# Batch norm over 32 x 256 x 128 x 128: the next load waits for VectorE, the next store for ScalarE

## The chip, the cores and the metric

The kernel runs on one core of a Trainium2 chip. The metric is the device time of one execution in microseconds (us), and the median of several runs is compared. Before the change it is 2484.73 us.

## What is computed

Batch normalisation with given statistics: a factor and an offset for each of 256 channels, applied to 32 images of 128 x 128.

```python
x:  (32, 256, 128, 128) float32        # 536.9 MB
gamma, beta, running_mean, running_var: (256,) float32

return gamma * (x - mean) / np.sqrt(var + eps) + beta     # eps = 1e-5, per channel
```

With `scale = gamma / sqrt(var + eps)` and `shift = beta - mean * scale`, each output is `x * scale + shift`. Each byte of `x` is read once and each byte of the result written once: 1073.7 MB in all.

## The kernel before

**Tiles.** `x` is cut into 64 tiles (32 images x 2 blocks of 128 channels). A tile has 128 partitions, one per channel, with 16384 columns of float32: 64 KB a partition, 8.39 MB in all. Three buffers (`NBUF = 3`) of that size lie in the on-chip memory, and tile i uses buffer i mod 3. A tile is loaded, changed in place, and stored from the same buffer.

**Loads** are issued by the sync engine (SP), on its own ring of DMA descriptors (q1 in the profile). Tile 0 comes in two pieces: a quarter (line 84), then the four rows of parameters (line 87), then the rest (line 91). Line 98 issues tile 1 right behind them, without a wait. Each later load i waits for two things: that the store of tile i - 3, which had the same buffer, has landed (line 97), and that load i - 1 has landed (line 100). So the load ring holds one transfer at a time from tile 2 on.

**The parameters** are turned and combined in a few small instructions at the start (lines 103 to 122); ScalarE's only part in it is a square root at line 111. At the end of it `scale_t` and `shift_t` stand ready, and VectorE waits for them at line 122.

**VectorE** computes a whole tile with one instruction (`compute`, line 126), as soon as its load has landed, and adds one to the semaphore `done`. Tile 0 takes two instructions, one for each piece.

**Stores** are issued by ScalarE (ACT), on a second ring (q10). Before the store of tile i, ScalarE waits until store i - 1 has landed (`turn_of_store`, line 141); the store itself waits for VectorE's count (line 138). So the store ring holds one transfer at a time too.

**The last tile** is shared: VectorE takes the first 9216 columns (`VCOLS`), ScalarE the other 7168 (line 154), both at once after the landing. Its store (line 161) does not wait for the store before, and so may stand behind it in the ring.

All waits are written out by hand with semaphores; nothing reorders them. `loaded[s]` and `stored[s]` count 16 for each transfer that has landed in, or left, buffer s.

Of the kernel before, what the change touches and what calls it, by code (L numbers as in the profile page):

```python
# [7 lines left out]

NBUF = 3

VCOLS = 9216


@with_exitstack
def kernel(
    ctx: ExitStack,
    tc: tile.TileContext,
    x: bass.AP,
    gamma: bass.AP,
    beta: bass.AP,  # L20
    running_mean: bass.AP,
    running_var: bass.AP,
    out: bass.AP,
):
    nc = tc.nc
    eps = 1e-5
    f32 = mybir.dt.float32

    N, C, H, W = x.shape
    P = nc.NUM_PARTITIONS  # L30
    assert C % P == 0
    NCB = C // P
    HW = H * W
    NT = N * NCB
    B = 32
    NQ = P // B
    NE = 16
    NPAR = 4

    xr = x.rearrange("n (cb p) h w -> (n cb) p (h w)", p=P)  # L40
    outr = out.rearrange("n (cb p) h w -> (n cb) p (h w)", p=P)

    params = ctx.enter_context(tc.tile_pool(name="params", bufs=1))
    data = ctx.enter_context(tc.tile_pool(name="data", bufs=1))
    bufs = [data.tile([P, HW], f32, name=f"t{s}", tag=f"t{s}") for s in range(NBUF)]
    rows = params.tile([B, NPAR * C], f32, name="rows", tag="rows")
    turned = params.tile([B, NPAR * C], f32, name="turned", tag="turned")
    par = params.tile([P, NPAR, NCB], f32, name="par", tag="par")
    eps_t = params.tile([P, 1], f32, name="eps_t", tag="eps")
    std_t = params.tile([P, NCB], f32, name="std_t", tag="std")  # L50
    rstd_t = params.tile([P, NCB], f32, name="rstd_t", tag="rstd")
    scale_t = params.tile([P, NCB], f32, name="scale_t", tag="scale")
    ms_t = params.tile([P, NCB], f32, name="ms_t", tag="ms")
    shift_t = params.tile([P, NCB], f32, name="shift_t", tag="shift")

    loaded = [tc.alloc_semaphore(f"loaded{s}") for s in range(NBUF)]
    stored = [tc.alloc_semaphore(f"stored{s}") for s in range(NBUF)]
    early = tc.alloc_semaphore("early")  # L60
    done = tc.alloc_semaphore("done")
    fetched = tc.alloc_semaphore("fetched")
    vec = tc.alloc_semaphore("vec")
    act = tc.alloc_semaphore("act")

    with tc.tile_critical():  # L66
        count = [0]

        def step(inst, sem=None, value=None):

            if sem is not None:
                inst._wait_ge(sem, value)
            elif count[0]:
                inst._wait_ge(vec, count[0])
            inst.then_inc(vec, 1)
            count[0] += 1
            return count[0]

        left, right = slice(0, HW // 4), slice(HW // 4, HW)
        last = NT - 1  # L80

        nc.sync.dma_start(out=bufs[0][:, left], in_=xr[0][:, left]).then_inc(early, 16)
        zeroed = step(nc.vector.memset(rows[:], 0.0))  # L85
        for r, ap in enumerate((running_var, gamma, beta, running_mean)):
            inst = nc.sync.dma_start(out=rows[0:NE, r * C : (r + 1) * C], in_=ap.partition_broadcast(NE))  # L87
            if r == 0:
                inst._wait_ge(vec, zeroed)
            inst.then_inc(fetched, 16)  # L90
        nc.sync.dma_start(out=bufs[0][:, right], in_=xr[0][:, right]).then_inc(loaded[0], 16)  # L91
        for i in range(1, NT):
            s, turn = i % NBUF, i // NBUF


            if turn:
                nc.sync.wait_ge(stored[s], 16 * turn)
            inst = nc.sync.dma_start(out=bufs[s][:], in_=xr[i]).then_inc(loaded[s], 16)
            if i >= 2:
                inst._wait_ge(loaded[(i - 1) % NBUF], 16 * ((i - 1) // NBUF + 1))  # L100


        step(nc.vector.memset(eps_t[:], eps))  # L103
        step(nc.vector.transpose(out=turned[:], in_=rows[:]), fetched, 16 * NPAR)  # L104

        blocks = turned.rearrange("p (rc q b) -> p rc q b", q=NQ, b=B)
        flat = par.rearrange("p r cb -> p (r cb)")
        for q in range(NQ):
            placed = step(nc.vector.tensor_copy(out=flat[q * B : (q + 1) * B], in_=blocks[:, :, q, 0]))  # L109
        var_t, gamma_t, beta_t, mean_t = (par[:, r] for r in range(NPAR))  # L110
        nc.scalar.activation(  # L111
            out=std_t[:],
            in_=var_t,
            func=mybir.ActivationFunctionType.Sqrt,
            bias=eps_t[:],
            scale=1.0,
        )._wait_ge(vec, placed).then_inc(act, 1)
        step(nc.vector.reciprocal(out=rstd_t[:], in_=std_t[:]), act, 1)  # L118
        step(nc.vector.tensor_mul(out=scale_t[:], in0=gamma_t, in1=rstd_t[:]))  # L119
        step(nc.vector.tensor_mul(out=ms_t[:], in0=mean_t, in1=scale_t[:]))  # L120
        ready = step(nc.vector.tensor_sub(out=shift_t[:], in0=beta_t, in1=ms_t[:]))  # L121
        nc.vector.wait_ge(vec, ready)

        def compute(i, cols=slice(0, HW)):
            t, cb = bufs[i % NBUF], i % NCB
            return nc.vector.tensor_scalar(  # L126
                out=t[:, cols],
                in0=t[:, cols],
                scalar1=scale_t[:, cb : cb + 1],
                scalar2=shift_t[:, cb : cb + 1],  # L130
                op0=mybir.AluOpType.mult,
                op1=mybir.AluOpType.add,
            ).then_inc(done, 1)

        def store(i, after):
            s = i % NBUF
            inst = nc.scalar.dma_start(out=outr[i], in_=bufs[s][:]).then_inc(stored[s], 16)
            inst._wait_ge(done, after)

        def turn_of_store(i):  # L140
            nc.scalar.wait_ge(stored[(i - 1) % NBUF], 16 * ((i - 1) // NBUF + 1))

        compute(0, left)._wait_ge(early, 16)
        compute(0, right)._wait_ge(loaded[0], 16)
        store(0, 2)
        for i in range(1, last):
            compute(i)._wait_ge(loaded[i % NBUF], 16 * (i // NBUF + 1))
            turn_of_store(i)
            store(i, i + 2)

        turns = last // NBUF + 1
        compute(last, slice(0, VCOLS))._wait_ge(loaded[last % NBUF], 16 * turns)
        t, cb = bufs[last % NBUF], last % NCB
        nc.scalar.activation(  # L154
            out=t[:, VCOLS:],
            in_=t[:, VCOLS:],
            func=mybir.ActivationFunctionType.Identity,
            bias=shift_t[:, cb : cb + 1],
            scale=scale_t[:, cb : cb + 1],
        )._wait_ge(loaded[last % NBUF], 16 * turns).then_inc(done, 1)  # L160
        store(last, last + 3)

        for s in range(NBUF):
            nc.sync.wait_ge(stored[s], 16 * ((NT - s + NBUF - 1) // NBUF))
# [30 lines left out]
```

## Time and profile before

| what | before |
|---|---|
| median of 5 runs | 2484.73 us (2483.59 to 2485.12) |
| the profiled execution: its time | 2485.12 us |
| the profiled execution: its span, first to last instruction | 2483.3 us |
| bytes moved by DMA | 1073.84 MB |
| VectorE busy | 564.1 us (23% of the span), 76 instructions |
| ScalarE busy | 7.9 us (0%), 3 instructions |
| a load, issue to landing, median (line 98) | 38.6 us |
| a store, issue to landing, median (line 137) | 38.6 us |
| share of the chain that ended last | DMA 99% |

The span leaves out what lies around the program, 1.8 us in this execution. The time of a load or a store in the table is that of a transfer that shares the 16 DMA engines with one of the other ring. In the views, SPq and ACTq are the queues of the sync engine and of ScalarE, from which DMAs are issued; DVE is VectorE, ACT ScalarE.

### The profile page before, as it was taken

Reading aid. Unit: us, or ns where it says so; the run is one execution under the profiler, and the core shown is the slowest. Engines: PE = TensorE matmul, PEld = TensorE weight load, DVE = VectorE, ACT = ScalarE, POOL = GpSimd, SP = SyncE. Lnnn points to the kernel's source line nnn. Section 1 sums busy time; section 2 is a strip of 40 time slices with the busy share of each in tenths; the row PEclk is TensorE's granted clock in tenths of the full one; section 3 lists DMA queues with packets and bytes.
Section 4 is the critical chain, followed back from the end, with each engine's and each line's share of the span. In section 5 each row is a group of like instructions: output and inputs, shape, how many; then the busy total and the mean of one; then the engine's idle time right before and its main releaser. Section 6 shows DMA issues by size and latency. Waiting matters only on the chain.

```text
span 2483.3 us, 389 instructions
## 1 busy us (share of the span) xinstructions
DVE 564.1 (23%) x76; ACT 7.9 (0%) x3; POOL 0.2 (0%) x4
## 2 busy tenths in 40 slices
DVE  3121221212212122122221222212212122121221
ACT  0000000000000000000000000000000000000001
POOL 0000000000000000000000000000000000000000
DMA  9999999999999999999999999999999999999999
GB/s 416 430 438 435 428 436 438 431 433 436 437 430 434 439 430 434 436 434 433 431 431 432 431 437 434 430 438 433 430 439 434 436 431 435 435 431 437 432 431 406
DMA packets 18707, 1073.84 MB, mean 432 GB/s; under 512 B 2128, under 2 KB 2192, under 8 KB 2192
## 3 DMA queue, kind: packets, MB, share of 16 engines
q1 hardware_dynamic: 9488, 536.94, 50.1%
q10 hardware_dynamic: 9216, 536.88, 49.9%
q14 instruction: 3, 0.02, 0.0%
HBM read 536.94 MB, written 536.87 MB: 432 GB/s over the span
## 4 chain that ended last, share of the span: by engine, by line
DMA 99%; ACT 0%; SPq 0%; issue 0%; DVE 0%; DVEq 0%
DMA t<-in_x_dram 99%; ACT t L154 0%; SPq L87 0%; DVE rows L85 0%; SPq L91 0%; DVE eps_t L103 0%; DVEq L190 0%; SPq L66 0%
## 5 line engine op out<-in xcount | busy, mean ns | idle before, releaser
L126 DVE TENSOR_SCALAR t<-t,scale_t,shift_t 128x16384 f32<-128x16384 f32 (+2 forms) x65 | 560.6, 8624 | 1885.0 <-DMA t<-in_x_dram 1884.9
L154 ACT ACTIVATE t<-t,shift_t,scale_t 128x7168 f32<-128x7168 f32 x1 | 6.4, 6362 | 2441.3 <-DMA t<-in_x_dram 2441.3
L104 DVE STREAM_TRANSPOSE turned<-rows 32x1024 f32<-32x1024 f32 x1 | 1.2, 1232 | 7.3 <-DMA rows<-in_running_mean_dram 7.3
L111 ACT ACT_TABLE_LOAD x1 | 1.3, 1283 | 0.9 <-SPq L66 0.9
L85 DVE MEMSET rows<- 32x1024 f32 x1 | 0.9, 912 | 1.2 <-SPq L66 1.2
L109 DVE COPY par<-turned 32x8 f32<-32x8 f32 x4 | 0.6, 162 | 0.1
L111 ACT ACTIVATE std_t<-par,eps_t 128x2 f32<-128x2 f32 x1 | 0.3, 295 | 9.4 <-DVE par L109 9.4
L118 DVE RECIPROCAL rstd_t<-std_t 128x2 f32<-128x2 f32 x1 | 0.2, 165 | 0.4 <-ACT std_t L111 0.4
L121 DVE TENSOR_TENSOR shift_t<-par,ms_t 128x2 f32<-128x2 f32 x1 | 0.2, 163 | 0.0
L120 DVE TENSOR_TENSOR ms_t<-par,scale_t 128x2 f32<-128x2 f32 x1 | 0.2, 161 | 0.0
L119 DVE TENSOR_TENSOR scale_t<-par,rstd_t 128x2 f32<-128x2 f32 x1 | 0.2, 160 | 0.0
L179 POOL MEMSET const-bfloat16-1.0<- 128x1 bf16 x1 | 0.1, 101 | 0.0
L179 POOL MEMSET const-uint8-127<- 128x1 uint8 x1 | 0.1, 101 | 0.0
L179 POOL MEMSET const-float32-0.0<- 128x1 f32 x1 | 0.1, 98 | 0.2 <-issue 0.2
L179 POOL MEMSET const-float32-1.0<- 128x1 f32 x1 | 0.1, 98 | 0.0
L103 DVE MEMSET eps_t<- 128x1 f32 x1 | 0.1, 59 | 0.1
## 6 DMA issues: line engine op xcount, KB each, us to landing
t<-in_x_dram SPq DMA_DIRECT2D x1, 6144.0 KB, 19.4
t<-in_x_dram SPq DMA_DIRECT2D x1, 2048.0 KB, 7.8
out_dram<-t ACTq DMA_DIRECT2D x64, 38.6
t<-in_x_dram SPq DMA_DIRECT2D x63, 38.6
rows<-in_running_var_dram SPq DMA_DIRECT2D x1, 16.0 KB, 6.2
rows<-in_gamma_dram SPq DMA_DIRECT2D x1, 16.0 KB, 6.0
rows<-in_beta_dram SPq DMA_DIRECT2D x1, 16.0 KB, 5.8
rows<-in_running_mean_dram SPq DMA_DIRECT2D x1, 16.0 KB, 6.0
```

Of the source, the lines that this page charges most:

```text
L85: zeroed = step(nc.vector.memset(rows[:], 0.0))
L103: step(nc.vector.memset(eps_t[:], eps))
L104: step(nc.vector.transpose(out=turned[:], in_=rows[:]), fetched, 16 * NPAR)
L109: placed = step(nc.vector.tensor_copy(out=flat[q * B : (q + 1) * B], in_=blocks[:, :, q, 0]))
L111: nc.scalar.activation(out=std_t[:], in_=var_t, func=mybir.ActivationFunctionType.Sqrt, bias=eps_t[:], scale=1.0,)._wait_ge(vec, placed).t ...
L118: step(nc.vector.reciprocal(out=rstd_t[:], in_=std_t[:]), act, 1)
L119: step(nc.vector.tensor_mul(out=scale_t[:], in0=gamma_t, in1=rstd_t[:]))
L120: step(nc.vector.tensor_mul(out=ms_t[:], in0=mean_t, in1=scale_t[:]))
L121: ready = step(nc.vector.tensor_sub(out=shift_t[:], in0=beta_t, in1=ms_t[:]))
L126: return nc.vector.tensor_scalar(out=t[:, cols], in0=t[:, cols], scalar1=scale_t[:, cb : cb + 1], scalar2=shift_t[:, cb : cb + 1], op0=myb ...
L154: nc.scalar.activation(out=t[:, VCOLS:], in_=t[:, VCOLS:], func=mybir.ActivationFunctionType.Identity, bias=shift_t[:, cb : cb + 1], scale ...
L179: nc = _bacc.Bacc("TRN2", target_bir_lowering=False, num_devices=1)
```

## The change

- **Loads.** Load i (from tile 2 on) no longer waits for the landing of load i - 1 itself, but for VectorE's first instruction on tile i - 1, which covers 2560 columns (`STEP`) and can start only after that landing. The wait for the buffer's store stays.
- **VectorE** works on a tile in two instructions: columns 0 to 2560, and 2560 to 14336 (`VCOLS`); each adds one to `vdone`. In the last tile the second one ends at column 9216 (`VLAST`).
- **ScalarE** computes the last 2048 columns of every tile (from the last tile 7168, as before). For tile i it waits until VectorE is done with the tile, and until store i - 1 has landed; then it computes its columns, adds one to `adone`, and the store of tile i waits for that.
- **Tile 0** comes in two halves instead of a quarter and the rest.

```diff
+STEP = 2560
+VCOLS = 14336
+VLAST = 9216
...
-        left, right = slice(0, HW // 4), slice(HW // 4, HW)
+        left, right = slice(0, HW // 2), slice(HW // 2, HW)
...
             inst = nc.sync.dma_start(out=bufs[s][:], in_=xr[i]).then_inc(loaded[s], 16)
             if i >= 2:
-                inst._wait_ge(loaded[(i - 1) % NBUF], 16 * ((i - 1) // NBUF + 1))
+                inst._wait_ge(vdone, 2 * (i - 1) + 1)
...
-        def compute(i, cols=slice(0, HW)):
+        def vector_part(i, first, end):
             t, cb = bufs[i % NBUF], i % NCB
             return nc.vector.tensor_scalar(
-                out=t[:, cols],
-                in0=t[:, cols],
+                out=t[:, first:end],
+                in0=t[:, first:end],
...
-            ).then_inc(done, 1)
+            ).then_inc(vdone, 1)
+
+        def scalar_part(i, first):
+            t, cb = bufs[i % NBUF], i % NCB
+            return nc.scalar.activation(
+                out=t[:, first:],
+                in_=t[:, first:],
+                func=mybir.ActivationFunctionType.Identity,
+                bias=shift_t[:, cb : cb + 1],
+                scale=scale_t[:, cb : cb + 1],
+            ).then_inc(adone, 1)
+
+        def landed(i):
+            return loaded[i % NBUF], 16 * (i // NBUF + 1)
+
+        def store(i):
             s = i % NBUF
-            inst = nc.scalar.dma_start(out=outr[i], in_=bufs[s][:]).then_inc(stored[s], 16)
-            inst._wait_ge(done, after)
...
+            nc.scalar.dma_start(out=outr[i], in_=bufs[s][:])._wait_ge(adone, i + 1).then_inc(stored[s], 16)
+
+        vector_part(0, 0, HW // 2)._wait_ge(early, 16)
+        vector_part(0, HW // 2, VCOLS)._wait_ge(*landed(0))
+        for i in range(1, NT):
+            vector_part(i, 0, STEP)._wait_ge(*landed(i))
+            vector_part(i, STEP, VLAST if i == last else VCOLS)
+        for i in range(last):
+            nc.scalar.wait_ge(vdone, 2 * (i + 1))
+            inst = scalar_part(i, VCOLS)
+            if i:
+                inst._wait_ge(stored[(i - 1) % NBUF], 16 * ((i - 1) // NBUF + 1))
+            store(i)
+        scalar_part(last, VLAST)._wait_ge(*landed(last))
+        nc.scalar.wait_ge(vdone, 2 * NT)
+        store(last)
```

## The prediction

> **What bounds the kernel now.** I read the page's counts first, then the chain of waits, the sync queue's own waits, short windows cut out of the steady part and out of both ends, and last the groups of instructions by shape. From the page, the rate over the span and the packets of the two queues (q1 carries loads, q10 stores):
>
> ```profile
> DMA packets 18707, 1073.84 MB, mean 432 GB/s; under 512 B 2128, under 2 KB 2192, under 8 KB 2192
> q1 hardware_dynamic: 9488, 536.94, 50.1%
> q10 hardware_dynamic: 9216, 536.88, 49.9%
> ```
>
> 64 stores make 9216 packets, 144 each: 128 rows of 64 KB and 16 of a few bytes. So each of the 16 DMA engines moves 8 rows of a store and 8 of a load per tile. The chain of waits (start, length, what) is nothing but loads, each issued 0.02 us after the one before:
>
> ```profile
> 479.59 38.59 DMA t<-in_x_dram
> 518.18 0.02 issue
> 518.20 38.64 DMA t<-in_x_dram
> ```
>
> A period of 38.6 us holds 16 rows per engine, so one row takes 38.63 / 16 = 2.414 us; I call that a **slot**. Whether an engine idles between transfers is seen in windows (start:end, length, busy time of DVE, ACT and POOL, a clock, DMA share, GB/s). In 90.70 to 95.53 the load ring changes tiles (a load is issued at 91.63); in 105.20 to 110.03 the store ring does:
>
> ```profile
> 90.70:95.53 4.83, 3.89 (x1) 0.00 (x0) 0.00 (x0) 1.00 1.00 434
> 105.20:110.03 4.83, 0.00 (x0) 0.00 (x0) 0.00 (x0) 1.00 1.00 434
> 1000.00:1038.63 38.63, 8.81 (x1) 0.00 (x0) 0.00 (x0) 1.00 1.00 434
> 2462.20:2479.10 16.90, 0.00 (x0) 0.00 (x0) 0.00 (x0) 1.00 1.00 434
> ```
>
> The reader is to see the same 434 GB/s in both changes, in a whole period, and at the end when a store runs alone. One ring alone fills the engines, and neither change of tile leaves them empty: the other ring takes the free slots. The kernel is bound by the sum of the bytes at 434 GB/s, and the loads' chain is only where the trace happens to follow it.
>
> **The ends of the span.** Until the first row arrives, and after the last one, nothing moves:
>
> ```profile
> 0.00:1.90 1.90, 0.68 (x1) 1.00 (x1) 0.20 (x4) 1.00 0.00 0
> 2481.80:2483.30 1.50, 0.00 (x0) 0.00 (x0) 0.00 (x0) 1.00 0.00 0
> ```
>
> 64 periods at 38.63 are 2472.3. In front stand 1.9; behind, the trace's packet records end the 16 engines' last rows between 2479.9 and 2481.7, on average 2480.5, which leaves 2.8 to the span's end. That explains 2477.0 of 2483.3; the other 6.3 are stragglers. The periods of loads from 52.97 to 2414.49 say the same: 61 of them average 38.71, while the shortest is 38.6, so 61 x 0.10 = 6.
>
> **The change, part by part.**
>
> Durations, by shape:
>
> ```profile
> L126 DVE TENSOR_SCALAR t<-t,scale_t,shift_t 128x16384 f32<-128x16384 f32 x62 | 546.4, 8813 | 1846.9 <-DMA t<-in_x_dram 1846.9
> L154 ACT ACTIVATE t<-t,shift_t,scale_t 128x7168 f32<-128x7168 f32 x1 | 6.4, 6362 | 2441.3 <-DMA t<-in_x_dram 2441.3
> L126 DVE TENSOR_SCALAR t<-t,scale_t,shift_t 128x4096 f32<-128x4096 f32 x1 | 2.4, 2415 | 0.1
> ```
>
> VectorE: (8813 - 2415) / 12288 = 0.521 ns a column and 282 ns fixed. So 2560 columns take 1.62 us, the other 11776 take 6.41, together 8.03 where 8.81 stood. ScalarE's 2048 columns: 2048/7168 of 6362 is 1.82; with the 0.295 us that a two-column ACTIVATE (L111) takes as fixed part it is 0.295 + 2048 x 0.000847 = 2.03. I take 2.0. One table load serves both functions of ScalarE in this trace, so none is added.
>
> 1. *The load waits for 2560 columns.* Its issue moves from 0.02 to about 0.02 + 1.62 + 0.03 = **1.67 us** after the landing, 62 times. Behind it on SP stands only the next load. Bounds: from -6.3, if the pause lets all stragglers catch up, over nothing, if the other ring fills it, to 62 x 1.67 = 104 us, if none of it is filled.
> 2. *The store waits for 2048 columns of ScalarE.* These start when the store before has landed, so the issue moves back by 2.0 plus two hand-overs, **2.1 us**, 62 times. Behind it on ScalarE stands the next tile's part, which waits for that same store anyway. Bounds: the same -6.3 for both parts together, nothing, or 62 x 2.1 = 130 us.
>
> Which end is nearer, the rows of the two changes of tile decide: a pause of two slots (4.83) was filled fully, 434 GB/s, on either ring. The first row of a transfer follows its issue by 1.0 us (issue at 0.95, nothing until 1.90, then 279 GB/s). If the engine chooses a row at a row's end, one slot ahead, a pause is 0.45 (in the packet records the engines' last rows of load 2 end from 90.78 to 91.24, and the landing is complete at 91.61) + issue delay + 1.0 to 1.5, rounded up to a slot, and one slot more. Before: 0.45 + 0.02 + 1.25 = 1.7, so 1 + 1 = 2 slots, as the trace shows. After: load 0.45 + 1.67 + 1.25 = 3.4, store 0.45 + 2.1 + 1.25 = 3.8; both lie between one slot (2.41) and two (4.83), so both pauses become **3 slots**. Two pauses of 3 fit in a period of 16 without meeting, and each row waited for on one ring is a row of the other done early. The period stays 16 slots = 38.63. I take **0** for parts 1 and 2. The cover is the other ring's transfer; where it is gone, a tile pays about 1.5 us and more (first rival).
>
> One rule of the Trainium skill speaks against the change: "DMA: Bandwidth & Descriptors", section "Rules for kernel authors", advises to issue a DMA early and wait late so that its fixed setup cost overlaps. Here the issue is put behind compute; by that rule alone the sum would gain the exposed 104 to 130 us, against 0 by the windows above.
>
> 3. *Buffers.* Nothing gets late as long as the sync queue reaches its wait for the landing last:
>
> ```profile
> SPq L98 <- DMA t<-in_x_dram: 1377.5, 62, 48.1
> SPq L97 <- DMA out_dram<-t: 1009.0, 61, 16.7
> ```
>
> The buffer of load i is free 1377.5 / 62 = **22.2 us** before the load may start. That is the spare. On the other side, VectorE is done 8.0 us after a landing and the store of that tile comes 16.5 us after it (1009.0 / 61): 8.5 spare.
>
> 4. *Tile 0.* Its left half is now 4 MB, so the parameters land 2 MB (4.8 us) later and shift_t is there at 12.65 + 4.83 = 17.5; 8192 columns take 4.55, to 22.0. The right half lands at 23.4 as before (same bytes before it), 6144 columns 3.48, ScalarE 2.0: store 0 at about 29.0 instead of 30.10. The load ring alone fills the engines then, so this is worth **0**.
>
> 5. *The end.* ScalarE's 7168 columns (6.36) after the last landing and the last store's issue are unchanged. Store 62 covers them: the engines ran at 437 GB/s from 2452.6 to 2462.2. If store 62 has one row less left, up to 2.4 - 1.5 = 1 us shows. I take **+0.3**.
>
> Sum: 2485.12 + 0 + 0 + 0 + 0.3 = 2485.4 by the profiled execution, which is 0.4 above the median of the runs. So **2485.0** beside 2484.73.
>
> **The rivals.**
>
> *A: The pauses stay hidden* (as worked out). 2485, own range 2480 to 2490. Chance 0.73.
>
> *B: Loads run into the stores' landing (slower).* Both delays differ by 0.43 us; the chance that a slot's edge lies between is about 0.43 / 2.41 = 0.18, less since both stand 1 us from it. With 3 slots for loads and 4 for stores, loads take (16 + 7) / (1 + 4/8) = 15.3 slots, stores (16 + 7) / (1 + 3/8) = 16.7: loads gain 1.4 slots = 3.4 us a tile. After 22.2 / 3.4 = 7 tiles the spare is used up. From then a load is issued as a store lands and both rings are empty together for 0.45 + 0.05 + 1.0 = 1.5 us, on 55 tiles: 82 us, **2567**. It decides once the sync queue's last wait is for a store. For it: ScalarE's part is the longer. Against: the rounding to slots, and that 62 tiles before kept one and the same distance. Chance 0.12.
>
> *C: Less spare between engines (slower).* Longer pauses leave an engine that ran ahead fewer rows of the other ring, so each straggler is paid by all engines. If the 6.3 us of stragglers cost twice or three times as much: 2491 to 2498, say **2493**. For it: one period of 39.91 beside 38.6. Against: such an excess is rare. Chance 0.08.
>
> *D: Stragglers go (faster).* A longer pause lets late engines catch up. All of it gone gives 2484.7 - 6.3 = **2478.4**; nothing can go below, as the rows are back to back. Chance 0.07, of which 0.04 past the 0.2% line.
>
> *That the change does nothing*: if both delays are swallowed by rounding, pauses stay 2 slots; the time is A's, and its chance is in A.
>
> **How the numbers follow.** 0.2% (5 us) is about what a measurement of this kernel can tell from no change. Faster: 0.04 from D. Slower: B 0.12 and C 0.08. Same: the rest, 0.76. The time is A's. The range takes A whole and C in most of its reach, 2480 to 2496, and leaves out B and the best of D.
>
> **What would show it.** In the profile after: load periods of 38.6 again; 434 GB/s in windows over both changes of tile; the sync queue waiting longest for VectorE or the landing, not for stores; 63 new ACTIVATE of about 2.0 us and VectorE groups of 1.62 and 6.41. B shows as a short or missing wait of the loads for the landing, periods of 40 us and a mean well under 432 GB/s; C as scattered long periods. Wrong would be the forecast if a period is other than 16 slots with both rings at work, above all if the rate in a shared period is not the same as alone.

## The result and the profile after

| what | before | after |
|---|---|---|
| median of the runs | 2484.11 us (60 runs) | 2497.13 us (34 runs) |
| ratio | | 1.0042, 95% interval 1.0034 to 1.0051 |
| how the runs lie | 59 from 2482.1 to 2487.8, one at 2510.1 | 7 from 2482.7 to 2486.5, 27 from 2495.1 to 2502.5, none between |

The change costs 0.4%, and not evenly: an execution is either as fast as before or some 11 us and more slower. The profile taken of the changed kernel is of one more execution, and caught the lower value (its time is 2483.82 us, its span 2482.0). It shows what was forecast. No execution of this kernel near 2497 was profiled; the profile of the first experiment has an upper value (2508). First the chain of waits (start, length, what) and the instructions by shape (busy, mean ns, idle before) of the changed kernel:

```profile
984.42 36.98 DMA t<-in_x_dram
1021.40 0.03 issue
1021.42 1.62 DVE t L130
1023.05 0.02 issue
1023.07 36.97 DMA t<-in_x_dram
```

```profile
L130 DVE TENSOR_SCALAR t<-t,scale_t,shift_t 128x11776 f32<-128x11776 f32 x62 | 397.2, 6407 | 0.0
L141 ACT ACTIVATE t<-t,shift_t,scale_t 128x2048 f32<-128x2048 f32 x63 | 131.8, 2093 | 2281.3 <-DMA out_dram<-t 2271.0 <-DVE t L130 10.4
L130 DVE TENSOR_SCALAR t<-t,scale_t,shift_t 128x2560 f32<-128x2560 f32 x63 | 101.6, 1612 | 1932.9 <-DMA t<-in_x_dram 1932.9
```

The chain now passes through VectorE's 1.62 us at every tile, and the load that follows is shorter by as much: 0.03 + 1.62 + 0.02 + 36.97 = 38.64, the period of before. The two new pieces of work last what was estimated (1.61 us on VectorE, 2.09 on ScalarE). Windows over the change of tile on the load ring, on the store ring, and over the long middle (columns as in the prediction) show where they went:

```profile
1020.00:1027.24 7.24, 5.82 (x2) 0.00 (x0) 0.00 (x0) 1.00 1.00 434
1034.00:1041.24 7.24, 0.00 (x0) 2.09 (x1) 0.00 (x0) 1.00 1.00 434
200.00:2400.00 2200.00, 452.29 (x114) 119.28 (x57) 0.00 (x0) 1.00 1.00 434
```

The rate is 434 GB/s in the pauses too. The sync queue waits where it did, with a little less spare on the stores' side (760.9 / 61 = 12.5 us where it waited 16.5):

```profile
SPq L102 <- DVE t L130: 1625.9, 62, 49.6
SPq L101 <- DMA out_dram<-t: 760.9, 61, 12.8
```

### The profile page after: what moved, and what is told of

It reads as the page before. It is cut to its first block, busy times and chain, and to the rows that moved or that the text cites. A ratio compares the mean times of both kernels' runs of the same rounds, so it can differ in the third digit from the quotient of the medians.

```text
span 2482.0 us, 516 instructions
## 1 busy us (share of the span) xinstructions
DVE 508.8 (20%) x139; ACT 139.8 (6%) x66; POOL 0.2 (0%) x4
## 3 DMA queue, kind: packets, MB, share of 16 engines
q10 hardware_dynamic: 9216, 536.88, 49.9%
## 4 chain that ended last, share of the span: by engine, by line
DMA 94%; DVE 4%; ACT 0%; issue 0%; SPq 0%; DVEq 0%
DMA t<-in_x_dram 94%; DVE t L130 4%; ACT t L141 0%; SPq L91 0%; DVE rows L89 0%; SPq L95 0%; DVE eps_t L107 0%; DVEq L198 0%; SPq L70 0%
## 5 line engine op out<-in xcount | busy, mean ns | idle before, releaser
L130 DVE TENSOR_SCALAR t<-t,scale_t,shift_t 128x11776 f32<-128x11776 f32 (+2 forms) x128 | 505.3, 3989 | 1934.5 <-DMA t<-in_x_dram 1934.3
L141 ACT ACTIVATE t<-t,shift_t,scale_t 128x2048 f32<-128x2048 f32 x64 | 138.2, 2159 | 2303.4 <-DMA out_dram<-t 2271.0
```

What stands on the lines that cost most here:

```text
L130: return nc.vector.tensor_scalar(out=t[:, first:end], in0=t[:, first:end], scalar1=scale_t[:, cb : cb + 1], scalar2=shift_t[:, cb : cb + 1 ...
L141: return nc.scalar.activation(out=t[:, first:], in_=t[:, first:], func=mybir.ActivationFunctionType.Identity, bias=shift_t[:, cb : cb + 1] ...
```

## The experiments

Two quantities are used below, both taken from the times at which the queues issue transfers. The **distance** of the rings is the time from a load's issue to the next store's issue: 16.9 us before the change, 14.9 in the profile just shown. The **period** is that between two loads between 200 and 2400 us. Ratios are to the kernel before on the same chip: e1 to e4 ran on one chip, e5 to e7 on a second, e8 and e9 on a third. The text also speaks of what one DMA engine did. The packet records (one record for each row of 64 KB) do not name the engine; a row is put on the engine whose row before it ended within a few nanoseconds of its start, which makes 16 unbroken chains.

### The changed kernel again, each delay alone, and tile 0 as before

`e1_after_again` is the changed kernel without an edit.

> The changed kernel once more, unchanged, for a second profile. Most of its executions were near 2497 us and a few near 2484, while its profiled execution had a span of 2482.0 and every pause of 3 slots hidden. Theory 1 (pauses meet): in a run near 2497 the rings drift until both are empty together for part of the run, so the mean rate falls below 432 GB/s in the middle, periods over 39 us stand in a row. Theory 2 (the end): the distance of the rings differs between executions, and store 62 ends before store 63 is ready; 10 to 13 us of engines without work stand in the last 40 us, the middle is as before.

`e2_load_only`: VectorE computes all columns, ScalarE only in the last tile. This also issues store 0 about 1 us earlier than in the changed kernel (28.06).

```diff
-        def store(i):
+        def store(i, sem, value):
             s = i % NBUF
-            nc.scalar.dma_start(out=outr[i], in_=bufs[s][:])._wait_ge(adone, i + 1).then_inc(stored[s], 16)
+            nc.scalar.dma_start(out=outr[i], in_=bufs[s][:])._wait_ge(sem, value).then_inc(stored[s], 16)
...
-        vector_part(0, HW // 2, VCOLS)._wait_ge(*landed(0))
+        vector_part(0, HW // 2, HW)._wait_ge(*landed(0))
...
-            vector_part(i, STEP, VLAST if i == last else VCOLS)
+            vector_part(i, STEP, VLAST if i == last else HW)
         for i in range(last):
-            nc.scalar.wait_ge(vdone, 2 * (i + 1))
-            inst = scalar_part(i, VCOLS)
             if i:
-                inst._wait_ge(stored[(i - 1) % NBUF], 16 * ((i - 1) // NBUF + 1))
-            store(i)
+                nc.scalar.wait_ge(stored[(i - 1) % NBUF], 16 * ((i - 1) // NBUF + 1))
+            store(i, vdone, 2 * (i + 1))
...
-        store(last)
+        store(last, adone, 1)
```

> Only the load waits for VectorE's 2560 columns; the store waits for the landing of the one before and for VectorE alone, ScalarE computes only in the last tile. Pauses: load 3 slots, store 2. Theory 1: stores gain on loads until they wait for VectorE; pauses do not meet then, 2485 within 3. If the load's delay alone is the cause, 2497 in most executions. Theory 2: the distance between the rings is changed, and the end with it: 2485 to 2497.

`e3_store_only`: the load waits for the landing alone, as before the change.

```diff
-                inst._wait_ge(vdone, 2 * (i - 1) + 1)
+                inst._wait_ge(loaded[(i - 1) % NBUF], 16 * ((i - 1) // NBUF + 1))
```

> Only the store waits for ScalarE's 2048 columns; the load waits for the landing, as before the change. Pauses: load 2 slots, store 3. Theory 1: loads gain 1 slot and more a tile until they wait for the stores' landing; from there both rings are empty together, 1.5 us a tile: up to 2567, with the sync queue waiting longest for stores. Theory 2: the middle stays at 38.63 a tile, only the end changes: 2485 to 2497.

`e4_tile0`: tile 0 in a quarter and the rest, as before the change.

```diff
-        left, right = slice(0, HW // 2), slice(HW // 2, HW)
+        left, right = slice(0, HW // 4), slice(HW // 4, HW)
...
-        vector_part(0, 0, HW // 2)._wait_ge(early, 16)
-        vector_part(0, HW // 2, VCOLS)._wait_ge(*landed(0))
+        vector_part(0, 0, HW // 4)._wait_ge(early, 16)
+        vector_part(0, HW // 4, VCOLS)._wait_ge(*landed(0))
```

> The changed kernel with tile 0 in a quarter and the rest, as before the change; both delays kept. Theory 1: the start has no part in it, 2497 in most executions again. Theory 2: store 0 comes at about another time, so the distance of the rings is another and stays: 2484 or 2497, but not the same mixture.

| kernel | median us, runs | ratio, 95% interval | period | distance |
|---|---|---|---|---|
| e1_after_again | 2507.64, 10 | 1.0074, 1.0056 to 1.0092 | 39.06 | 10.1 |
| e2_load_only | 2579.11, 4 | 1.0363, 1.0341 to 1.0385 | 40.30 | 7.4 |
| e3_store_only | 2714.96, 4 | 1.0909, 1.0893 to 1.0925 | 42.58 | 2.1 |
| e4_tile0 | 2486.48, 10 | 0.9993, 0.9983 to 1.0002 | 38.73 | 15.0 |

**e4 finds the part that costs.** With tile 0 in a quarter and the rest, and both delays kept, all 10 runs lie between 2485.0 and 2488.7. With this start the delays as a pair are free; with the halves of tile 0, on the same chip, 9 of 10 runs of e1 are near 2508. This is against what theory 1 said of it.

**e1 shows the slower execution** (its profiled time is 2508.28; one of its 10 runs was 2486.88). Its chain of waits has the same links as the changed kernel above, only longer loads:

```profile
1033.50 1.62 DVE t L130
1035.12 0.02 issue
1035.14 37.55 DMA t<-in_x_dram
1072.69 0.03 issue
1072.72 1.62 DVE t L130
```

Here a period is 39.22. Windows of the same execution:

```profile
1031.00:1038.24 7.24, 4.74 (x2) 0.00 (x0) 0.00 (x0) 1.00 1.01 434
1043.00:1055.10 12.10, 0.00 (x0) 2.09 (x1) 0.00 (x0) 1.00 1.01 417
200.00:2400.00 2200.00, 444.39 (x112) 117.18 (x56) 0.00 (x0) 1.00 1.00 429
```

The DMA share is full, yet the rate is 429 GB/s over the middle, and 417 around the time at which stores begin after a pause. So theory 2 (the end) falls: the loss is spread over the middle. Theory 1 holds only in part. Periods over 39 us do stand in a row (34 of 55), but no engine is without work: single rows take longer. In the packet records the row is 2.418 us long as a rule; the excess over that, between 200 and 2400 us, comes to 0.42 us a tile on each engine, all of it on loads, against 0.03 in the profile at 2483.82 and 0.08 in that of e4. e1 and e4 ran on one chip: 0.42 - 0.08 over 62 tiles is 21 us, and their spans (2506.5 and 2486.0) differ by 20.5.

Where the two executions of one program part is seen at the start. The changed kernel at 2483.82, then e1 at 2508.28, in order of time (start, length, engine, line):

```profile
29.09 0.37 ACTq L154 DMA_DIRECT2D out_dram<-t  x1
52.84 7.94 DVE L130 TENSOR_SCALAR t<-t,scale_t,shift_t 128x2560 f32<-128x2560 f32 x2 [25.91 <-DMA t<-in_x_dram]
69.48 0.34 ACTq L154 DMA_DIRECT2D out_dram<-t  x1
```

```profile
29.13 0.38 ACTq L154 DMA_DIRECT2D out_dram<-t  x1
55.13 7.94 DVE L130 TENSOR_SCALAR t<-t,scale_t,shift_t 128x2560 f32<-128x2560 f32 x2 [28.15 <-DMA t<-in_x_dram]
67.43 0.34 ACTq L154 DMA_DIRECT2D out_dram<-t  x1
```

Store 0 is issued 0.04 us apart, but load 1 lands 2.29 us later in the second (the VectorE lines) and store 1 is issued 2.05 earlier: the rings have come nearer by nearly two slots. The packet records say why. In e1 one engine of the 16 started its row of the store at 32.92, the other 15 between 35.0 and 35.7; in the execution at 2483.82 all 16 started between 35.0 and 35.6. That one engine began its row before at 30.36, 1.23 us after the store's issue; the others began theirs at 30.19 or earlier, 1.06 us and less. In the execution at 2483.82 one engine began a row 1.21 us after the issue and still went on with a load. This reads as an engine that decides on a row's start what it will do next, with the store in reach some 1.2 us after its issue; the figure is not the same on every engine. In e4 engines that began a row 1.10 us after the issue took the store, while in e6 one at 1.53 and in e2 one at 1.82 went on with loads. One engine in time for the earlier slot seems to be enough: its load row comes a slot later, a landing is that of the slowest engine, and load 2 waits for the landing.

e4 fits this, and shows that a split among the engines does no harm by itself. Its store 0 is issued at 31.21; 8 engines start their row of it between 35.1 and 35.7, the other 8 a slot later, near 38. The earliest slot is the one that all engines had in the execution at 2483.82, the distance is the same 15 us, and all ten runs are near the value of before.

**e3 is rival B in the chip.** Pauses of 2 slots on loads and 3 on stores: the first loads come every 36.3 us and the first stores after 41.2, the rings drift apart, and the sync queue ends up waiting for stores.

```profile
SPq L101 <- DMA out_dram<-t: 2474.1, 61, 43.1
SPq L102 <- DMA t<-in_x_dram: 125.8, 7, 50.3
```

2474.1 of 2715.7 us are waits for a store, and a period costs 42.58 - 38.63 = 3.95 us more. The waiting was forecast, the price was not: the expectation was up to 2567. In the packet records an engine stands 2.4 us a tile without a row, and its load rows take 1.6 us longer in all.

**e2 missed its expectation** in part: stores gained on loads, as written, until they waited for VectorE, but that is not free. The timeline:

```profile
1025.36 9.00 DVE L130 TENSOR_SCALAR t<-t,scale_t,shift_t 128x2560 f32<-128x2560 f32 x2 [32.63 <-DMA t<-in_x_dram]
1027.00 38.78 SPq L102 DMA_DIRECT2D t<-in_x_dram  x2
1034.39 39.41 ACTq L154 DMA_DIRECT2D out_dram<-t  x2
```

VectorE is done at 1025.36 + 9.00 = 1034.36, and the store is issued 0.03 us later. The store ring is empty while it waits for the tile that has just landed, which is also when the load ring is between tiles; a period takes 40.30. Of the 1.6 us by which that is longer than in the changed kernel, an engine stands 0.35 without a row; 1.3 are longer rows of loads.

### Store 0 later, earlier, and the halves without the delays

If it is the slot that store 0 meets, moving its issue by a few tenths of a microsecond decides the time of the whole kernel. `e5_store0_later` and `e6_store0_earlier` change only the split of tile 0 between VectorE and ScalarE, with `VFIRST` 12288 and 15360:

```diff
+VFIRST = 12288
...
-        vector_part(0, HW // 2, VCOLS)._wait_ge(*landed(0))
+        vector_part(0, HW // 2, VFIRST)._wait_ge(*landed(0))
...
-            inst = scalar_part(i, VCOLS)
+            inst = scalar_part(i, VCOLS if i else VFIRST)
```

> The changed kernel, with the halves of tile 0, where ScalarE takes 4096 columns of tile 0 instead of 2048 and VectorE 2048 fewer; tiles 1 to 63 as changed. Store 0 is issued some 0.7 us later, near 29.8. Theory (slot edge): in the slow execution one engine only had its store row one slot (2.41 us) earlier than the other 15, because it chose its next row at 30.36, 1.2 us after the issue at 29.13; with the issue at 29.8 no engine is in time for that slot. Then all executions are near 2485, the rings stand 15 us apart (store issue after load issue) and periods are 38.65. Rival (halves): what costs is that the parameters land later or the first load is larger; then 2497 to 2508 in most executions, as with the changed kernel.

> The changed kernel, where ScalarE takes 1024 columns of tile 0 instead of 2048 and VectorE 1024 more; tiles 1 to 63 as changed. Store 0 is issued some 0.4 us earlier, near 28.7. Theory (slot edge): most engines now choose the store's row a slot earlier; load 1 lands a slot later, the rings stand some 10.5 us apart in all executions, load rows take longer after each lone stretch, and all executions are at the upper value, 2497 to 2508. Rival (halves): no difference from the changed kernel, both values in a mixture.

`e7_halves_alone` is the kernel before with the halves:

```diff
-        left, right = slice(0, HW // 4), slice(HW // 4, HW)
+        left, right = slice(0, HW // 2), slice(HW // 2, HW)
```

> The kernel before with the halves of tile 0 alone: no delay of loads or stores. Store 0 is issued near 28.0. Theory (slot edge, and pauses that touch): the rings move 2 slots nearer, some 12 us apart, but pauses of 2 slots leave room between them: 2485, at most 2488. Rival (halves): 2495 to 2508.

| kernel | store 0 issued | engines in the earlier slot | distance | median us, runs | ratio, 95% interval |
|---|---|---|---|---|---|
| after, 2483.82 | 29.09 | 0 | 14.9 | | |
| e1, 2508.28 | 29.13 | 1 | 10.1 | | |
| e5_store0_later | 29.61 | 0 | 15.0 | 2484.77, 10 | 0.9996, 0.9986 to 1.0005 |
| e6_store0_earlier | 28.79 | 4 | 10.1 | 2497.18, 4 | 1.0050, 1.0035 to 1.0065 |
| e7_halves_alone | 28.01 | 16 | 12.1 | 2485.69, 10 | 1.0004, 0.9994 to 1.0014 |

The issue of store 0 in e5 and in e6, from the timelines:

```profile
29.61 0.38 ACTq L155 DMA_DIRECT2D out_dram<-t  x1
```

```profile
28.79 0.38 ACTq L155 DMA_DIRECT2D out_dram<-t  x1
```

Half a microsecond later, and all 10 runs are at the value of before (2482.2 to 2487.6); 0.3 us earlier, and all 4 are at the upper one (2496.7 to 2498.7). The profile of e6 (2498.69) is the nearest on record to an execution at 2497, and it has the distance of e1. The halves stand in both, so they cost nothing by themselves; they only put store 0 on the edge. The count of engines in e6 was expected to be most of the 16 and was 4 in the profiled execution; one is enough, as e1 shows. In e7 all 16 engines are in the earlier slot and nothing is lost: with the shorter pauses of the kernel before, a shorter distance (12.1 us) is free. This loss was seen only where near rings and longer pauses came together.

### Longer pauses, with store 0 kept late

What near rings and longer pauses have in common is that a pause of one ring ends where the pause of the other begins. Two kernels lengthen the pauses and keep store 0 late. `e8_pauses_4_4` is e5 with `STEP = 7168` and `VCOLS = 12288`; `e9_pauses_3_4` is e5 with `VCOLS = 12288` alone:

```diff
-STEP = 2560
+STEP = 7168
 VFIRST = 12288
-VCOLS = 14336
+VCOLS = 12288
```

> As e5_store0_later (store 0 near 29.6, the rings 15 us apart at the start), but the load waits for 7168 columns of VectorE (4.0 us) and the store for 4096 of ScalarE (3.8 us) on every tile: by the slot rule both pauses are 4 slots instead of 3. Theory (pauses that touch cost): with 4 and 4 no mixed row is left between the end of one pause and the start of the other, load rows take longer again: 2495 or more, at most 2560. Rival (only the distance at the start counts, or the prediction's rule that pauses stay hidden while they fit in 16 slots): 2485.

> As e5_store0_later, but ScalarE takes 4096 columns of every tile (3.8 us) and the load waits for 2560 columns as in the change: load pauses of 3 slots, store pauses of 4. This is the prediction's rival B, priced at 2567: loads gain some 3.4 us a tile until they wait for the stores' landing, from about tile 9, and both rings are empty together. If pauses of unequal length are what drifts, as with e3_store_only (2 and 3 slots, 2715), the sync queue's longest wait is for stores and the time is 2567 to 2715. Rival (length of the delay counts, not the difference in slots): near e8.

| kernel | median us, runs | ratio, 95% interval | period | distance |
|---|---|---|---|---|
| e8_pauses_4_4 | 2499.52, 4 | 1.0064, 1.0047 to 1.0081 | 38.92 | 11.9 |
| e9_pauses_3_4 | 2648.36, 2 | 1.0661, 1.0640 to 1.0682 | 41.49 | |

In e8 the chain shows a wait for VectorE of 4.02 us at every tile, taken back by shorter loads almost fully:

```profile
1029.52 4.02 DVE t L131
1033.54 0.02 issue
1033.56 35.02 DMA t<-in_x_dram
1068.58 0.03 issue
1068.60 4.02 DVE t L131
```

Although no engine of e8 takes store 0 in the earlier slot, its distance is not 15 us: with longer pauses it stands at e7's (11.9 and 12.1). It has 38.92 a period where e7 has 38.69, so it is not the distance alone. To see what it is, I counted in the packet records how often, on one engine between 200 and 2400 us, a run of three or more rows of stores is followed at once by three or more rows of loads. That is, how often no mixed row is left between the two pauses:

```
kernel              pauses touch   excess of load rows, us a tile and engine
before                    0%            0.06
after at 2483.82         56%            0.03
e4_tile0                 57%            0.08
e5_store0_later          59%            0.05
e7_halves_alone          69%            0.05
e6_store0_earlier        98%            0.25
e8_pauses_4_4            98%            0.28
e1_after_again          100%            0.42
```

Up to 69% the excess stays under 0.1 us; from 98% on a tile costs 0.25 to 0.42 us. So the loss goes with pauses that touch on nearly all engines. That touching is its cause is not shown: no run lies between 69% and 98%, and the longer rows do not stand at the touch. In e1, 91% of the excess falls on load rows that start within 9.7 us after a store is issued, that is, where the lone loads end and stores begin; those that start 2.4 to 4.8 us after the issue are 0.41 us longer on average. Why they take longer, while the store rows of these eight kernels do not, is left open; no run here separates the memory from the engines.

e9 shows that a difference between the two pauses, not their length, makes the large loss: it has shorter load pauses than e8 and takes 149 us more. The sync queue waits for stores again:

```profile
SPq L102 <- DMA out_dram<-t: 2055.6, 61, 35.1
SPq L103 <- DVE t L131: 482.2, 62, 50.0
```

An engine of e9 stands 0.8 us a tile without a row; rows of loads take 1.3 us a tile longer in all, and here rows of stores do too, by 0.8.

No kernel tried is clear of the one before on the faster side. e4 and e5 come nearest, and their intervals hold 1.

## Why the prediction was right and where it was wrong

- **The bound.** Right. Bytes at 434 GB/s set the time, and a sole ring keeps the engines full. Nothing went below the time of before, as the prediction argued.
- **The delays and the slot rule.** Right. The delays were forecast at 1.67 and 2.1 us and both pauses at 3 slots. The profile after has 1.67 (0.03 + 1.62 + 0.02) and 2.09 for ScalarE's work alone, periods of 38.64, and 434 GB/s in both pauses. The rows agree with the rule: between a ring's last row and its next, an engine does at least 3 rows of the other ring before the change, 4 after and, in nearly all cases, 5 in e8, that is the 2, 3 and 4 slots and the one row that alternates anyway. That delays are rounded is seen in the distance, which stays between 14.9 and 15.1 us from 200 to 2400 us although the store's delay is some 0.4 us the longer. What a slot's difference costs is shown by e2, e3 and e9: 91, 227 and 164 us against the kernel before on the same chip. e3's 227 is more than the 130 us that the prediction named as the most that its delay could cost. One reading of the prediction is off by a row, without harm to the rule: what ends from 90.78 to 91.24 are the packets of a few bytes that close load 2; its last rows of 64 KB ended at 88.4 to 88.8.
- **"Two pauses of 3 fit in a period of 16 without meeting."** Incomplete. They fit, and no engine idles, yet where they touch on nearly all engines rows of loads take longer. The prediction took the time of a row as fixed, 2.414 us. This is the term that was missing: 0.25 to 0.42 us a tile in e6 and e1, less the 0.05 to 0.08 of e5 and e4 on the same chips, so 12 to 21 us in all.
- **Step 4, tile 0, "worth 0".** This is the step that failed. Its times were right (store 0 at 29.0 forecast, 29.09 measured; shift_t at 17.5, VectorE starts at 17.49). Its reading was not: it asked only whether the load ring alone fills the engines, not which slot store 0 then meets, though its own estimate (first row 1.0 to 1.5 us after the issue, a choice one slot ahead) was enough to ask. The issue at 29.1 puts the arrival at the last engine's edge, 30.3: an engine that began a row at 30.30 went on with a load and the run took 2483.82, one that began at 30.36 took the store and the run took 2508.28. On the chip of e1 this one engine goes with some 21 us (one of its ten runs took 2486.88).
- **The forecast.** "Same" at 2485 describes 7 of 34 executions. The median, 2497.13, is just over the upper end of 2496, while the ratio puts the change at 0.42%, inside it. That the range reaches so far is luck: its upper part was there for rival C, whose cause did not occur. By the prediction's own line of 0.2% the kernel got slower, and slower had a chance of 0.2.
- **Rival B** did not happen in the change, since both pauses round to 3 slots. Its mechanism is real, and its price was too low. It was put at 1.5 us a tile; e9, its exact case, pays 41.49 - 38.63 = 2.9, and e3 3.95. The prediction counted only the time without any row, which is 0.8 in e9 and 2.4 in e3; the rest is rows that take longer.
- **Rival C** came nearest in size (2493), by the wrong cause: not a few long stragglers, but a loss spread over most periods (in e1 34 of 55 are over 39 us, against 2 of 56 in the profile at 2483.82).
- **The skill's advice.** The Trainium skill ("DMA: Bandwidth & Descriptors", section "Rules for kernel authors") advises to issue a DMA early and to wait for it late. By that rule alone the prediction priced the change at 104 to 130 us. With both delays together the kernel pays nothing of that (e4, e5); with one alone it pays 91 (e2) and 227 us (e3), and there the advice points the right way.

## What to carry to other kernels

Where the two DMA rings shared engines that never ran dry, a delay of one ring was free only if the other ring's pause rounded to the same number of rows, and not always then (e1, e6, e8); change both or neither, and count pauses in rows, not in microseconds. The place in time of the first transfer on the second ring can set the order for the whole run: look at the earliest row that any engine gives it, and keep its issue some tenths of a microsecond away from a point where one engine takes it a row earlier than the others did. A time that falls on two values from run to run asks for the profile of both.

## What the runs showed of the hardware

- A busy engine does not turn to a new transfer as soon as its present row ends: in e1, engines that started a row 1.06 us or less after the issue of store 0 did another load row after it, and the one that started at 1.23 us did the store's row next. On other engines and in other profiles that point lay between 1.1 us (e4) and over 1.8 us (e2).
- In two executions of one program whose first store row differs on one engine of 16, the distances of the rings differ by two slots (14.9 and 10.1 us) and stay so from 200 to 2400 us: 2483.82 and 2508.28 us (the chip of the first is not on record).
- In e1, e6 and e8, where stores alone are followed at once by loads alone on nearly all engines, load rows take longer around the next start of stores (0.41 us on average in e1 for those that start 2.4 to 4.8 us after a store's issue), while store rows stay at 2.418 us. The price is not the same each time: the upper value of the changed kernel was near 2497 in the first comparison and near 2507.5 in e1.
